# Attention scores on one core: loads issued from ScalarE's DMA queue, stores from SyncE's

## The chip, the cores and the metric

The kernel runs on one core of a Trainium2 chip. The metric is the device time of one execution in microseconds (us). The profile's span is some 2 us shorter than that time, as it leaves out what lies before the first and after the last instruction.

A profile names the engines PE (TensorE), PEld (its weight loads), DVE (VectorE), ACT (ScalarE), POOL (GpSimd) and SP (SyncE). Sixteen DMA engines move the data. "SPq" and "ACTq" are the sequencers that issue DMAs. L56 is line 56 of the kernel.

## The reference

```python
batch, heads, seq, dim = 8, 8, 512, 64          # q, k: float32
scale = 1.0 / np.sqrt(dim)
out = np.einsum('bhqd,bhkd->bhqk', q, k) * scale   # float32, (8, 8, 512, 512)
```

The inputs are 16.8 MB, the output 67.1 MB: a problem of stores.

## The kernel before

Each batch is loaded with two DMAs of 1 MB, four batches ahead. Its tiles are cast to bf16, transposed on PE, multiplied, and the scores are scaled out of PSUM, the memory that PE writes to, by ACT and DVE in turn, into output tiles of 2 MB. Six of these are in flight.

```python
raw_pool = ctx.enter_context(tc.tile_pool(name="raw", bufs=4))
out_pool = ctx.enter_context(tc.tile_pool(name="out", bufs=6))
AHEAD = 4

def load(b):
    kf = raw_pool.tile([P, 2, R * D], f32, name="kf")
    qf = raw_pool.tile([P, 2, R * D], f32, name="qf")
    nc.sync.dma_start(out=kf, in_=k_r[b])
    nc.sync.dma_start(out=qf, in_=q_r[b])
    raws[b] = (qf, kf)

load(0)
# ... identity for the transposes
for b in range(1, AHEAD):
    load(b)
# ...
for b in range(B):
    qf, kf = raws.pop(b)
    # ... casts (POOL; for b = 0 DVE and ACT), transposes, copies to kT (DVE), qT (ACT)
    for g0 in range(0, G, 2):                      # two groups a batch
        os = [out_pool.tile([P, 2 // HP, RO, S], f32, name="o") for _ in range(2)]
        # ... matmuls; evacuations alternate between ACT and DVE
        for x in range(2):
            nc.sync.dma_start(out=out_r[b, x, ...], in_=os[x]...)   # cut
        if g0 == 0 and b + AHEAD < B:
            load(b + AHEAD)
```

Of the kernel before, what the change touches and what calls it, by code (L numbers as in the profile page):

```python
# [1 line left out]

# [5 lines left out]


@with_exitstack  # L10
def kernel(
    ctx: ExitStack,
    tc: tile.TileContext,
    q: bass.AP,
    k: bass.AP,
    out: bass.AP,
):





    nc = tc.nc
    B, H, S, D = q.shape
    scale = 1.0 / (D ** 0.5)
    P = 128
    G = H // 2
    M = P // G
    R = S // M
    RO = 8  # L30
    HP = RO * P // S
    U = P // HP
    JJ = R // RO

    f32 = mybir.dt.float32
    bf16 = mybir.dt.bfloat16

    q_r = q.rearrange("b (x g) (m j) d -> b (g m) x (j d)", x=2, j=R)
    k_r = k.rearrange("b (x g) (m j) d -> b (g m) x (j d)", x=2, j=R)
    out_r = out.rearrange("b (x n h) (u i) k -> b x n (h u) i k", x=2, h=HP, i=RO)  # L40

    consts = ctx.enter_context(tc.tile_pool(name="consts", bufs=1))
    raw_pool = ctx.enter_context(tc.tile_pool(name="raw", bufs=4))
    bf_pool = ctx.enter_context(tc.tile_pool(name="bf", bufs=2))
    t_pool = ctx.enter_context(tc.tile_pool(name="t", bufs=2))
    out_pool = ctx.enter_context(tc.tile_pool(name="out", bufs=6))
    tpsum_pool = ctx.enter_context(tc.tile_pool(name="tpsum", bufs=2, space=bass.MemoryType.PSUM))
    psum_pool = ctx.enter_context(tc.tile_pool(name="psum", bufs=3, space=bass.MemoryType.PSUM))

    AHEAD = 4  # L50
    raws = {}

    def load(b):
        kf = raw_pool.tile([P, 2, R * D], f32, name="kf")
        qf = raw_pool.tile([P, 2, R * D], f32, name="qf")
        nc.sync.dma_start(out=kf, in_=k_r[b])  # L56
        nc.sync.dma_start(out=qf, in_=q_r[b])
        raws[b] = (qf, kf)

    load(0)  # L60
    identity = consts.tile([P, P], dtype=bf16)
    make_identity(nc, identity)
    for b in range(1, AHEAD):
        load(b)

    n_evac = 0

    def evacuate(dst, src):
        nonlocal n_evac
        if n_evac % 2 == 0:  # L70
            nc.scalar.mul(out=dst, in_=src, mul=scale)  # L71
        else:
            nc.vector.tensor_scalar(out=dst, in0=src, scalar1=scale, scalar2=None,  # L73
                                    op0=mybir.AluOpType.mult)
        n_evac += 1

    for b in range(B):
        qf, kf = raws.pop(b)
        kb = bf_pool.tile([P, R, 2, D], bf16, name="kb")
        qb = bf_pool.tile([P, R, 2, D], bf16, name="qb")  # L80
        for slab, dst in ((kf, kb), (qf, qb)):
            for x in range(2):
                if b > 0:
                    copy = nc.gpsimd.tensor_copy
                else:
                    copy = (nc.vector.tensor_copy, nc.scalar.copy)[x]
                copy(out=dst[:, :, x, :], in_=slab[:, x].rearrange("p (j d) -> p j d", j=R))  # L87


        kT = t_pool.tile([P, P, R], bf16, name="kT")  # L90
        qT = t_pool.tile([P, RO, P, JJ], bf16, name="qT")
        for j0 in range(0, R, 8):
            tp = tpsum_pool.tile([P, 8, P], bf16, name="tp")
            for j in range(8):
                nc.tensor.transpose(out=tp[:, j, :], identity=identity,  # L95
                                    in_=kb[:, j0 + j].rearrange("p x d -> p (x d)"))
            nc.vector.tensor_copy(out=kT[:, :, j0:j0 + 8], in_=tp.rearrange("d j p -> d p j"))  # L97
        IW = 8 // JJ
        for i0 in range(0, RO, IW):
            tp = tpsum_pool.tile([P, IW, JJ, P], bf16, name="tp")  # L100
            for i in range(IW):
                for jj in range(JJ):
                    nc.tensor.transpose(out=tp[:, i, jj, :], identity=identity,  # L103
                                        in_=qb[:, RO * jj + i0 + i].rearrange("p x d -> p (x d)"))
            nc.scalar.copy(out=qT[:, i0:i0 + IW], in_=tp.rearrange("d i jj p -> d i p jj"))  # L105

        kTh = kT.rearrange("d (g m) j -> d g (m j)", g=G)
        qTh = qT.rearrange("d i (g m) jj -> d i g (m jj)", g=G)
        for g0 in range(0, G, 2):
            os = [out_pool.tile([P, 2 // HP, RO, S], f32, name="o") for _ in range(2)]  # L110
            for n in range(2 // HP):
                for i in range(0, RO, 2):
                    pss = [psum_pool.tile([P, 2, S], f32, name="ps") for _ in range(2)]
                    for w in range(2):
                        for h in range(HP):
                            g = g0 + n * HP + h
                            for x in range(2):
                                rows = slice(x * D, (x + 1) * D)
                                nc.tensor.matmul(out=pss[x][h * U:(h + 1) * U, w, :],  # L119
                                                 lhsT=qTh[rows, i + w, g, :],  # L120
                                                 rhs=kTh[rows, g, :],
                                                 start=True, stop=True,
                                                 tile_position=(x * D, h * U))
                    for x in range(2):
                        evacuate(os[x][:, n, i:i + 2, :], pss[x])
            for x in range(2):
                n0 = g0 // HP
                nc.sync.dma_start(  # L128
                    out=out_r[b, x, n0:n0 + 2 // HP].rearrange("n p i k -> p n (i k)"),
                    in_=os[x].rearrange("p n i k -> p n (i k)"))  # L130
            if g0 == 0 and b + AHEAD < B:
                load(b + AHEAD)


# [1 line left out]
_INS = ['q', 'k']  # L136
_OUTS = [((8, 8, 512, 512), 'float32')]


# [23 lines left out]
```

## Time and profile before

| | before |
|---|---|
| time, median of 4 runs | 206.03 us |
| span of the profiled run | 204.0 us |
| PE / DVE / ACT / POOL busy | 63% / 46% / 41% / 14% |
| packets of the one data queue, share of 16 DMA engines' time | 97.6% |
| first and last of the last store's 16 completions | 198.7 and 203.2 us |

The prediction shows the lines that this rests on. The last row needs a word. A DMA is spread over the 16 DMA engines, and each reports when its part is done, so a DMA has 16 completions. The **lag** of an engine is how far its completion of the last store lies behind the first one. I sort the 16 completion times of the last store, which the trace records. They don't tell which engine is which.

### The profile page before, as it was taken

To read this page: it belongs to the slowest core of one execution; us is meant where nothing else is said; L and a number is where in the kernel's file an instruction comes from. 1 tells how busy PE (TensorE), PEld (TensorE's weight loads), DVE (VectorE), ACT (ScalarE), POOL (GpSimd) and SP (SyncE) were. 2 spreads that over 40 slices of the span, in tenths; PEclk is the share of its full clock that TensorE was granted. 3 is DMA by queue.
4 is the path that set the end of the run, shared out by engine and by line. 5 is a ranking of instruction groups with operands and counts; after the bars stand their busy time and mean duration, and the time that the engine had idled before them with its cause. 6 is when DMAs were issued, how large, how long until landed. Compare 5 with 4: busy or idle time off the path is not lost.

```text
span 204.0 us, 1911 instructions
## 1 busy us (share of the span) xinstructions
PE 128.7 (63%) x768; PEld 44.1 (22%) x768; DVE 94.4 (46%) x82; ACT 82.8 (41%) x83; POOL 29.0 (14%) x34
## 2 busy tenths in 40 slices
PE   0398877774969559696586955959787777600000
PEld 0353433260103411033110431103211111000000
DVE  0459895912639035490536705367628081800000
ACT  2477888263522625227252452527552525200000
POOL 1077530520006100070001600000000000000000
PEclk9999999666555855558555575555555555555555
DMA  5999999999999999999999999999999999999991
GB/s 204 419 409 411 439 427 404 441 434 424 437 400 432 440 421 419 434 429 427 440 407 414 438 427 437 427 421 437 424 430 437 426 434 424 430 437 427 434 408 61
DMA packets 8969, 84.01 MB, mean 412 GB/s; under 512 B 768, under 2 KB 768, under 8 KB 4864
## 3 DMA queue, kind: packets, MB, share of 16 engines
q1 hardware_dynamic: 8960, 83.89, 97.6%
q8 instruction: 6, 0.10, 0.2%
q14 instruction: 3, 0.02, 0.0%
HBM read 16.78 MB, written 67.11 MB: 411 GB/s over the span
## 4 chain that ended last, share of the span: by engine, by line
DMA 61%; DVE 14%; PE 6%; ACT 6%; issue 1%; SPq 0%; DVEq 0%
DMA out_dram<-o 57%; DVE o L73 11%; PE ps L119 4%; ACT o L71 4%; DMA qf<-in_q_dram 3%; DVE kT L97 3%; ACT qT L105 1%; PE tp L103 1%; PE tp L95 0%; DVE qb L87 0%; SPq L56 0%; SPq L128 0%; DVEq L73 0%
## 5 line engine op out<-in xcount | busy, mean ns | idle before, releaser
L119 PE MATMUL ps<-kT,qT 64*64 64x512 bf16 x512 | 103.1, 556 | 38.6 <-ACT o L71 24.9
L73 DVE TENSOR_SCALAR o<-ps 128x1024 f32<-128x1024 f32 x64 | 75.2, 1219 | 76.7 <-DMA out_dram<-o 56.8
L71 ACT ACTIVATE o<-ps 128x1024 f32<-128x1024 f32 x64 | 64.5, 1025 | 77.1 <-PE ps L119 65.7
L119 PEld LDWEIGHTS <-qT 64*64 64x64 bf16 x512 | 22.4, 124 | 111.5 <-issue 108.6
L87 POOL CAST kb<-kf 128x1024 bf16<-128x1024 f32 x14 | 14.2, 1040 | 80.9 <-DMA kf<-in_k_dram 80.3
L105 ACT COPY qT<-tp 128x1024 bf16<-128x1024 bf16 x16 | 16.1, 1015 | 12.6 <-PE tp L103 12.4
L97 DVE COPY kT<-tp 128x1024 bf16<-128x1024 bf16 x16 | 18.9, 1215 | 0.0
L95 PE MATMUL tp<-identity,kb 128*128 128x128 bf16 x128 | 12.4, 257 | 8.0 <-ACT kb L87 6.9
L103 PE MATMUL tp<-identity,qb 128*128 128x128 bf16 x128 | 14.9, 284 | 2.2 <-DVE kT L97 1.4
L87 POOL CAST qb<-qf 128x1024 bf16<-128x1024 f32 x14 | 14.2, 1040 | 6.4 <-DMA qf<-in_q_dram 6.4
L103 PEld LDWEIGHTS <-qb 128*128 128x128 bf16 x128 | 11.7, 130 | 9.6 <-issue 8.6
L95 PEld LDWEIGHTS <-kb 128*128 128x128 bf16 x128 | 10.4, 118 | 11.4 <-ACT kb L87 6.9
L87 DVE CAST kb<-kf 128x1024 bf16<-128x1024 f32 x1 | 0.7, 694 | 5.8 <-DMA kf<-in_k_dram 5.8
L87 ACT CAST kb<-kf 128x1024 bf16<-128x1024 f32 x1 | 1.0, 1044 | 3.8 <-DMA kf<-in_k_dram 3.8
L87 ACT CAST qb<-qf 128x1024 bf16<-128x1024 f32 x1 | 1.0, 1044 | 1.5 <-DMA qf<-in_q_dram 1.5
L87 ACT ACT_TABLE_LOAD x1 | 1.3, 1283 | 0.7 <-PEq L147 0.7
L87 DVE CAST qb<-qf 128x1024 bf16<-128x1024 f32 x1 | 0.7, 695 | 1.9 <-DMA qf<-in_q_dram 1.9
masks.py:199 POOL TENSOR_SCALAR_AFFINE_SELECT identity<-identity 128x128 bf16<-128x128 bf16 x1 | 0.3, 292 | 0.1
masks.py:197 POOL MEMSET identity<- 128x128 bf16 x1 | 0.2, 204 | 0.3 <-POOLq L147 0.3
L147 POOL MEMSET const-float32-0.0<- 128x1 f32 x1 | 0.1, 98 | 0.2 <-issue 0.2
L147 POOL MEMSET const-bfloat16-1.0<- 128x1 bf16 x1 | 0.1, 101 | 0.0
L147 POOL MEMSET const-uint8-127<- 128x1 uint8 x1 | 0.1, 101 | 0.0
(1 smaller groups left out, 0.1 us busy)
## 6 DMA issues: line engine op xcount, KB each, us to landing
out_dram<-o SPq DMA_DIRECT2D x32, 2048.0 KB, 24.8
kf<-in_k_dram SPq DMA_DIRECT2D x8, 1024.0 KB, 17.2
qf<-in_q_dram SPq DMA_DIRECT2D x8, 1024.0 KB, 19.6
```

What stands on the lines that cost most here:

```text
L71: nc.scalar.mul(out=dst, in_=src, mul=scale)
L73: nc.vector.tensor_scalar(out=dst, in0=src, scalar1=scale, scalar2=None, op0=mybir.AluOpType.mult)
L87: copy(out=dst[:, :, x, :], in_=slab[:, x].rearrange("p (j d) -> p j d", j=R))
L95: nc.tensor.transpose(out=tp[:, j, :], identity=identity, in_=kb[:, j0 + j].rearrange("p x d -> p (x d)"))
L97: nc.vector.tensor_copy(out=kT[:, :, j0:j0 + 8], in_=tp.rearrange("d j p -> d p j"))
L103: nc.tensor.transpose(out=tp[:, i, jj, :], identity=identity, in_=qb[:, RO * jj + i0 + i].rearrange("p x d -> p (x d)"))
L105: nc.scalar.copy(out=qT[:, i0:i0 + IW], in_=tp.rearrange("d i jj p -> d i p jj"))
L119: nc.tensor.matmul(out=pss[x][h * U:(h + 1) * U, w, :], lhsT=qTh[rows, i + w, g, :], rhs=kTh[rows, g, :], start=True, stop=True, tile_posi ...
L147: nc = _bacc.Bacc("TRN2", target_bir_lowering=False, num_devices=1)
```

## The change

Loads go to another issuer. The intent of such a change is that loads don't wait behind stores in one queue, and that SyncE has stores alone.

```diff
     def load(b):
         kf = raw_pool.tile([P, 2, R * D], f32, name="kf")
         qf = raw_pool.tile([P, 2, R * D], f32, name="qf")
-        nc.sync.dma_start(out=kf, in_=k_r[b])
-        nc.sync.dma_start(out=qf, in_=q_r[b])
+        nc.scalar.dma_start(out=kf, in_=k_r[b])
+        nc.scalar.dma_start(out=qf, in_=q_r[b])
         raws[b] = (qf, kf)
```

The compiler's scheduler then also reorders the instructions around these loads on ACT, DVE and PE.

## The prediction

> **What bounds the kernel now.** I read the page's slices first, then the DMA queues, the chain that ended last, the waits, the first 8 us of SyncE's queue, and last the packets and landings themselves.
>
> ```profile
> span 204.0 us, 1911 instructions
> ...
> PE 128.7 (63%) x768; PEld 44.1 (22%) x768; DVE 94.4 (46%) x82; ACT 82.8 (41%) x83; POOL 29.0 (14%) x34
> ...
> DMA  5999999999999999999999999999999999999991
> ...
> q1 hardware_dynamic: 8960, 83.89, 97.6%
> ...
> HBM read 16.78 MB, written 67.11 MB: 411 GB/s over the span
> ...
> DMA 61%; DVE 14%; PE 6%; ACT 6%; issue 1%; SPq 0%; DVEq 0%
> ```
>
> No compute engine is above 63%, and PE is at 63% partly because its clock is at half speed. The row of DMA is 9 from the second slice to the last but one: the 16 DMA engines never go empty in between. All loads and stores are on one queue, q1, whose packets fill 97.6% of the time of 16 engines. The chain confirms it: 61% is DMA. The rest (DVE 14%, PE and ACT 6% each) is compute that was itself let go by a store's buffer coming free, as the waits of the engines show:
>
> ```profile
> POOL kb L87 <- DMA kf<-in_k_dram: 80.3, 6, 20.0
> ...
> DVE o L73 <- DMA out_dram<-o: 56.8, 11, 8.7
> ...
> ACT o L71 <- DMA out_dram<-o: 11.1, 8, 1.7
> ```
>
> Compute waits for transfers, not transfers for compute. (POOL's 80.3 us is POOL having nothing to do; it reads far ahead of need.)
>
> How full are the DMA engines really? From the packets in the trace: 4096 load packets of 4 KB with a median of 159 ns, 4096 store packets of 16 KB with a median of 611 ns, and 768 completion packets of 9 ns. Each engine has a sixteenth: 256 x 0.159 = 40.7 us, 256 x 0.611 = 156.4 us, 48 x 0.009 = 0.4 us, in all 197.5 us. The first packet starts at 1.83 us, so an engine that never pauses ends at 199.4 us. The last store's 16 completions, one an engine, come from 198.7 to 203.2 us. So the least disturbed engine runs its packets without a gap, and the slowest is some 4.5 us behind it. The last windows (us, five engines, granted clock, DMA share, GB/s) show that tail:
>
> ```profile
> 192.00:196.00 4.00, 0.00 (x0) 0.00 (x0) 0.00 (x0) 0.00 (x0) 0.00 (x0) 0.50 0.99 426
> 196.00:200.00 4.00, 0.00 (x0) 0.00 (x0) 0.00 (x0) 0.00 (x0) 0.00 (x0) 0.50 0.76 324
> 200.00:204.00 4.00, 0.00 (x0) 0.00 (x0) 0.00 (x0) 0.00 (x0) 0.00 (x0) 0.50 0.10 41
> ```
>
> Part of that lag comes from packets that are not the kernel's data: six instruction fetches of 16 KB (queue q8) of about 1 us each, on whichever engine gets them. The floor of the kernel is thus 1.8 us of start, 197.5 us of packets, about 4 us of the slowest engine's lag, and 0.8 us after its completion: 204.
>
> **What the Trainium skill says.** "DMA: Bandwidth & Descriptors", section "Issuing engines are not separate DMA queues": DMAs from the scalar, sync or gpsimd engine run on the same 16 engines and interleave; several issuers only save the sequencer's time. The trace of before has one issuer and cannot test this, but it says that there is little issuing time to save: SyncE's queue has a median of 0.34 us for a store's issue beside 4.9 us that its 2 MB take. The same page, "Queues, rings and completion order": each engine goes round its queues packet by packet. No run here shows that yet for two data queues; it would mean that a 4 KB load packet alternates with a 16 KB store packet. "Where 436 GB/s comes from" gives a ceiling of 435 GB/s; the windows from 48 us on mostly show 418 to 442, agreeing within the way packets are counted by their start. Against these stands "Perfetto Trace Analysis", "DMA Optimizations", which says that an issuer for inputs and another for outputs may make sense, for a more dynamic spread. That pays where one waits behind the other while the DMA engines are idle, which the DMA row rules out here.
>
> **The change, part by part.**
>
> Nothing is removed: 16 loads of 1 MB and 32 stores of 2 MB, the same packets of the same sizes. The 197.5 us of packets stay.
>
> (a) The first eight loads move to ScalarE's queue. On SyncE they went like this (start, us, instruction):
>
> ```profile
> 0.74 0.43 SPq L56 DMA_DIRECT2D kf<-in_k_dram  x1
> ...
> 4.05 0.94 SPq L56 DMA_DIRECT2D kf<-in_k_dram  x1
> 5.03 2.28 SPq L57 DMA_DIRECT2D qf<-in_q_dram  x1
> ```
>
> The first begins at 0.74; ScalarE, whose first instruction (the table load) began at 0.73, can begin as early: no change of the first packet. The last one is held until 7.31, I think for room in the queue. ScalarE now does this in front of its table load (1.28 us), since the compiled order puts the eight issues first. So its first cast begins at about 7.3 + 1.3 = 8.6 us in place of 5.82: 2.8 us late. Its next load stands before the first qT copy, with a wait on POOL, at worst for the casts of batch 1 (10.96 + 2.02 = 13.0), and the one after that before the first evacuation, at worst until 13.52 + 2.02 = 15.5. The first ScalarE evacuation goes from 13.5 to about 16, and the first store from 18.9 to 21 to 22.5 us.
>
> Does the start delay the end? Only if the DMA engines run dry. The eight loads last until 8 x 2.56 + 2.8 = 23.3 us (2.56 us is the distance of two landings, 8.3 to 10.9), and the two loads issued by 16 us bring it to 28.4. That is 6 us after the first store. So 0 us.
>
> (b) The eight later loads leave SyncE's order, where each stood behind stores waiting for evacuations, and go into ScalarE's. Eight issues of about 0.4 us are 3.2 us, plus waits for buffers and for the semaphores that are shared by DMAs, on an engine that is busy 82.8 of 204 us. In the middle of the kernel ScalarE is held by full output buffers anyway. 0 us on the path.
>
> (c) Loads share the engines with stores instead of lying between them. With a 4 KB packet for each 16 KB packet, a load gets 159/(159 + 611) = 21% of the time while both wait. A batch of 2 MB then takes 5.1/0.21 = 24 us, an estimate. They are issued earlier than before, four batches ahead, so they land in time. Order changes, sums don't: 0 us.
>
> (d) The only place where the sum can move is the packet itself. The two medians give (611 - 159)/12288 = 0.0368 ns a byte and about 8 ns a packet that isn't data. If a second queue hid these 8 ns for the packets that overlap (about 128 loads and 128 stores an engine), it would save at most 2 us. If going from queue to queue costs as much, it loses 2 us. I see nothing for either sign.
>
> (e) The lag of the slowest engine depends on which engine fetches instructions when; the total stays, the spread can change by one fetch, 1 us.
>
> Sum: 0 us, give or take some 2. **206.0 us.**
>
> **The rivals.**
>
> *Loads get out of the stores' way and the kernel gains.* Before, POOL waits up to 20.0 us for a load, and ScalarE and DVE wait for stores. For it: loads are issued earlier. Against it: the DMA row has no hole to fill. Only the tail of about 4 us and the start are not full, and the change reaches neither. At best 202 to 203, still within 2%.
>
> *ScalarE becomes the bottleneck.* A load that waits in its stream holds evacuations, and a ring that is full holds them longer (the longest issue of a load was 2.28 us, of a store 4.29 us). For it: eight more such waits of 2 to 4 us are 16 to 32 us of ScalarE, in the stretch up to some 80 us. Against it: 82.8 + 32 = 115 of 204 us, and six output buffers of 2 MB are up to 29 us of stores in hand. If the stall came early, before stores pile up, the DMA engines could stop for 2 to 5 us: 208 to 211.
>
> *Mixing reads and writes packet by packet is slower.* In the mixed stretch, up to perhaps 100 us, packets of both kinds would take 3 to 5% longer, which is 3 to 5 us: 209 to 211. Before, loads and stores meet only at the borders, where the trace shows load packets of 160 to 163 ns on average in most windows, so little speaks for it.
>
> **Range and chances.** The floor holds from both sides, and the unknowns are (d), (e) and a stall at the start. Range 204.3 to 208.6. Faster by over 2% (under 201.9) would need the lag of the slowest engine gone: 0.02. Slower by over 2% (over 210.1) needs a rival at its full size: 0.05. Same: 0.93.
>
> **What the changed kernel's profile will show.** Two data queues, of 16.8 and 67.1 MB, again some 97% of 16 engines together; a DMA row of 9s; the first ScalarE cast at 8 to 9 us and the first store at 21 to 23; later loads that land before they are needed; the last store's completions spread over 3 to 5 us. A DMA row with an 8 or less between 20 and 45 us would show the early stall; a full row with a longer span and medians above 159 and 611 would show the mixing; a span shorter by more than 4 us would show that I took for a floor what is none.

## The result, and the profile after

The time is 205.25 us (205.13 to 205.38, 4 runs). The ratio to before is 0.996, with a 95% interval of 0.9942 to 0.9977. A ratio here is the mean time of one kernel's runs over that of the other's of the same rounds, so not quite the ratio of the medians quoted. The verdict is "same" at 2%, as predicted, but a gain of 0.8 us stands clear of the noise, and I had predicted none.

The page after:

```profile
span 203.2 us, 1910 instructions
...
PE 129.5 (64%) x768; PEld 46.5 (23%) x768; DVE 95.2 (47%) x82; ACT 81.9 (40%) x83; POOL 29.0 (14%) x34
...
DMA  6999999999999999999999999999999999999991
...
q1 hardware_dynamic: 4608, 67.11, 77.3%
q10 hardware_dynamic: 4352, 16.78, 20.7%
...
DMA 51%; DVE 17%; PE 14%; ACT 2%; POOL 1%; issue 1%; ACTq 1%; SPq 0%; DVEq 0%
```

The stores are alone on q1, the loads on q10, and their shares add up to 98.0%. The DMA row is as full as before. The medians of the packets are the same to the nanosecond, 159 and 611.

ACT's timeline (start, us, instruction, and what it had waited for) shows the late start that was forecast:

```profile
0.73 0.42 ACTq L56 DMA_DIRECT2D kf<-in_k_dram  x1
...
4.76 2.38 ACTq L57 DMA_DIRECT2D qf<-in_q_dram  x1
7.17 1.28 ACT L87 ACT_TABLE_LOAD   x1 [7.17 <-issue]
8.46 1.04 ACT L87 CAST kb<-kf 128x1024 bf16<-128x1024 f32 x1
...
15.80 1.94 ACT L71 ACTIVATE o<-ps 128x1024 f32<-128x1024 f32 x2 [0.66 <-PE ps L119]
```

The first cast is at 8.46 us, the first evacuation at 15.80, and the first store is issued at 23.10. None of this reaches the end of the kernel.

The end itself, in the windows of the changed kernel (us, five engines, the clock granted to TensorE as a share of full speed, DMA share, GB/s):

```profile
192.00:196.00 4.00, 0.00 (x0) 0.00 (x0) 0.00 (x0) 0.00 (x0) 0.00 (x0) 0.50 0.98 418
196.00:200.00 4.00, 0.00 (x0) 0.00 (x0) 0.00 (x0) 0.00 (x0) 0.00 (x0) 0.50 0.75 320
200.00:204.00 4.00, 0.00 (x0) 0.00 (x0) 0.00 (x0) 0.00 (x0) 0.00 (x0) 0.50 0.03 12
```

Up to 200 us these are the lines of before: 0.99, 0.76. Only the last differs, 0.03 for 0.10. The bulk of the DMA engines ends when it did; a few laggards end earlier. From the trace, the 16 lags of the last store in us:

```
before  0  .1 .2 .2 .3 .3 .4 1.0 1.0 1.5 1.5 1.6 2.5 2.9 3.6 4.5   first 198.7, sum 21.4
after   0  0  .1 .1 .1 .2 .2  .5  .8 1.4 1.5 1.5 1.5 1.6 1.7 3.7   first 198.8, sum 15.0
```

So the whole 0.8 us is the slowest DMA engine's lag, 3.7 for 4.5. The mean engine ends at 198.7 + 21.4/16 = 200.0 before and at 198.8 + 15.0/16 = 199.7 after.

Where was the mean's 0.3 us taken? Among the load packets. Leaving out the first 3 us and counting what packets of over 190 ns took beyond 159, there are 31 such packets with 6.2 us together before, and 8 with 1.3 us after. The difference of 4.9 us, over 16 engines, is 0.3 us: nearly the whole difference of the mean. The slowest engine's 0.8 us is another matter; it is traced after the experiments. Before, apart from some at 3 and 22 us, they stand at 36 to 37, 60 to 62, 86 to 87 and 107 to 113 us, where loads come after stores in the one queue.

**A surprise in the middle.** The queue of SyncE in the changed kernel (waited for: us in total, times, longest us):

```profile
SPq L128 <- ACT o L71: 109.2, 14, 12.4
SPq L128 <- DMA qf<-in_q_dram: 29.4, 3, 19.2
...
SPq L128 <- DMA kf<-in_k_dram: 18.0, 3, 10.0
```

Stores waited for loads, up to 19.2 us, although no store needs a load's data directly. The waits in the compiled program show why: each DMA uses one of eight DMA semaphores in turn, both queues share them, and a store waits until the earlier DMA of its semaphore, here a load, has landed. The windows between 56 and 72 us show what this did (engines as above):

```profile
56.00:60.00 4.00, 2.42 (x25) 0.98 (x26) 1.96 (x2) 1.62 (x2) 0.72 (x1) 0.99 0.99 409
60.00:64.00 4.00, 2.41 (x12) 0.54 (x12) 0.00 (x0) 2.37 (x3) 3.32 (x4) 0.50 1.04 429
64.00:68.00 4.00, 0.63 (x4) 0.00 (x0) 0.00 (x0) 0.00 (x0) 0.00 (x0) 0.50 1.01 429
68.00:72.00 4.00, 0.75 (x4) 0.18 (x4) 2.03 (x2) 0.00 (x0) 0.00 (x0) 0.50 1.03 437
```

From 57.5 to 62.5 us there were 498 load packets and 2 store packets: the stores were held, and the loads took the engines whole. From 64 to 72 compute almost stood still, because its output buffers came free later. The DMA share stayed at 1.0 all along, so it cost nothing.

### The profile page after: what moved, and what is told of

Same layout as the page of the kernel before. It is cut to its first block, busy times and chain, and to the rows that moved or that the text cites. A ratio compares the mean times of both kernels' runs of the same rounds, so it can differ in the third digit from the quotient of the medians.

```text
span 203.2 us, 1910 instructions
## 1 busy us (share of the span) xinstructions
PE 129.5 (64%) x768; PEld 46.5 (23%) x768; DVE 95.2 (47%) x82; ACT 81.9 (40%) x83; POOL 29.0 (14%) x34
## 4 chain that ended last, share of the span: by engine, by line
DMA 51%; DVE 17%; PE 14%; ACT 2%; POOL 1%; issue 1%; ACTq 1%; SPq 0%; DVEq 0%
DMA out_dram<-o 36%; DVE o L73 13%; DMA qf<-in_q_dram 11%; PE ps L119 10%; DVE kT L97 5%; DMA kf<-in_k_dram 4%; PE tp L95 2%; PE tp L103 2%; ACT o L71 2%; POOL kb L87 1%; ACT qT L105 1%; ACTq L56 0%; ACTq L57 0%; SPq L128 0%; DVEq L73 0%
## 5 line engine op out<-in xcount | busy, mean ns | idle before, releaser
L119 PE MATMUL ps<-kT,qT 64*64 64x512 bf16 x512 | 101.8, 584 | 35.2 <-DVE o L73 17.1
L119 PEld LDWEIGHTS <-qT 64*64 64x64 bf16 x512 | 24.0, 131 | 94.8 <-issue 91.7
L95 PE MATMUL tp<-identity,kb 128*128 128x128 bf16 x128 | 14.8, 277 | 9.6 <-ACT kb L87 9.6
L103 PE MATMUL tp<-identity,qb 128*128 128x128 bf16 x128 | 16.4, 297 | 2.5 <-DVE kT L97 1.9
L103 PEld LDWEIGHTS <-qb 128*128 128x128 bf16 x128 | 12.3, 136 | 12.5 <-issue 11.6
```

What stands on the lines that cost most here:

```text
L95: nc.tensor.transpose(out=tp[:, j, :], identity=identity, in_=kb[:, j0 + j].rearrange("p x d -> p (x d)"))
L103: nc.tensor.transpose(out=tp[:, i, jj, :], identity=identity, in_=qb[:, RO * jj + i0 + i].rearrange("p x d -> p (x d)"))
L119: nc.tensor.matmul(out=pss[x][h * U:(h + 1) * U, w, :], lhsT=qTh[rows, i + w, g, :], rhs=kTh[rows, g, :], start=True, stop=True, tile_posi ...
```

## The experiments

The theory to start with, A: the DMA engines are the bound, and only the lag of the slowest one, made by stray packets such as instruction fetches, moves the time. The rival B: two data queues as such are worth 0.4%. Twelve kernels ran, in three sets and one single; the kernels of a set ran on the same chip.

### Parts of the change, and a control

e1 swaps the issuers, e2 and e3 move only some of the loads, e4 keeps one queue but loads q ahead of k.

```diff
 # e1_swap
-                nc.sync.dma_start(     # the store
+                nc.scalar.dma_start(
 # e2_first8
-        nc.sync.dma_start(out=kf, in_=k_r[b])      # qf likewise
+        dq = nc.scalar if b < AHEAD else nc.sync
+        dq.dma_start(out=kf, in_=k_r[b])
 # e3_later8: as e2, with b >= AHEAD
 # e4_q_first
-        nc.sync.dma_start(out=kf, in_=k_r[b])
         nc.sync.dma_start(out=qf, in_=q_r[b])
+        nc.sync.dma_start(out=kf, in_=k_r[b])
```

> Loads from SyncE, stores from ScalarE: two data queues again, other issuers. Theory A (the lag of the slowest DMA engine, and it alone, sets the difference; it comes from where single extra packets such as instruction fetches fall, and any rearrangement moves it): first completion of the last store at 198.7 +- 0.3 us as in both kernels, the last one 3 to 5 us later, time 204.5 to 206.5. Rival B (two data queues as such are worth 0.4%): time 205.2, ratio 0.996, lag below 4 us like the changed kernel. Rival C (ScalarE's sequencer is hurt when it issues under full queues): over 207.

> Only the first eight loads from ScalarE: ScalarE starts late as in the changed kernel, but loads and stores never lie on two queues at the same time for long. Theory A: fast engine ends at 198.7, lag anywhere in 3 to 5 us, 204.5 to 206.5. Rival B: 206.0 (no gain, as two queues are not active together). Rival D (the late start of ScalarE costs time at the end): 207 to 209.

> Only the later eight loads from ScalarE. Rival B: 205.2, as the two queues are active together as in the changed kernel. Theory A: 204.5 to 206.5, with the first completion of the last store at 198.7 +- 0.3 and the time following the lag of the slowest engine.

> Control: one queue (SyncE) as before, but q is loaded ahead of k. No second queue, the same bytes and packets. Theory A: the time moves by up to 1 us either way although the queue is one, and the lag of the slowest engine moves with it. Rival B: 206.0 within 0.1%, ratio 1.000, lag 4.5 us.

| kernel | time, us | ratio (95%) | later loads share a queue with stores | excess of load packets over 190 ns after 30 us | first completion, slowest lag |
|---|---|---|---|---|---|
| e1_swap | 206.12 | 0.9998 (0.9977 to 1.0019) | no | 1.0 us | 202.1, 1.8 |
| e2_first8 | 205.80 | 0.9989 (0.9974 to 1.0004) | yes | 1.3 us | 199.1, 4.0 |
| e3_later8 | 205.56 | 0.9977 (0.9962 to 0.9992) | no | 0.6 us | 198.7, 3.5 |
| e4_q_first | 205.98 | 1.0001 (0.9983 to 1.0019) | yes | 5.4 us | 198.8, 4.5 |
| before | 206.05 | | yes | 4.8 us | 198.7, 4.5 |

The control e4 does not move: it has the lag of before, 4.5, and the long packets of before. That speaks against the part of A by which any rearrangement shifts the time, and for B. (The last fetch of e4 comes when that of before came, as shown below, so e4 is no test of fetches.) e3 has a gain with only the later loads moved; e2's gain is not clear of zero. In this table little excess is mostly faster and much is not, but e2 doesn't fit: it has little, and a lag of 4.0. The last part of this section says why. The count starts at 30 us; e1 has another 28 long load packets with 4.5 us at 20 to 24 us, where its stores begin beside its loads. And e1 has two queues as well and gains nothing. Its profiled run is the slowest of its six (206.67 us). The page and two windows show another loss:

```profile
DMA  5999999999999999999989999999999999999994
...
96.00:100.00 4.00, 1.85 (x12) 0.53 (x12) 0.76 (x1) 2.93 (x4) 0.00 (x0) 0.50 0.92 389
100.00:104.00 4.00, 3.60 (x29) 1.70 (x25) 1.80 (x3) 2.67 (x3) 0.00 (x0) 0.50 0.66 281
```

Here the DMA engines ran dry, with a share of 0.66 from 100 to 104 us. What ACT waited for (us in total, times, longest) tells why it was late with its work:

```profile
ACT o L71 <- DMA out_dram<-o: 17.5, 1, 17.5
ACT qT L105 <- DMA kf<-in_k_dram: 14.3, 1, 14.3
```

ACT, which had to evacuate, stood behind its own store issues, one of which waited for a load's semaphore. This is the rival "ScalarE becomes the bottleneck" of the prediction, and with stores on ACT it is real. Yet it cost little. The first completion comes 3.4 us later than before (202.1), but the lag is 1.8 in place of 4.5: while the fast engines had nothing, the slow ones caught up. The largest lag of a store was 2.0 us at 97 us, and 0.2 at 109. A pause in the middle is paid for with lag, up to the lag that would have been there.

### Transfers alone

e5 and e6 keep the loads and stores and drop everything else; the stores read one cleared tile. Their outputs are wrong, which doesn't matter for the times. e7 is the real kernel with 128 tiny memsets a batch on POOL, which was meant to add instruction fetches.

```diff
 # e5_dma_one; e6_dma_two: the same with nc.scalar in load()
+    src = consts.tile([P, 2 // HP, RO, S], f32)
+    nc.vector.memset(src, 0.0)
-            # casts, transposes, matmuls, evacuations
-                    in_=os[x].rearrange(...))
+                    in_=src.rearrange(...))
 # e7_pool
+        for _ in range(128):
+            nc.gpsimd.memset(scratch, 0.0)
         kT = t_pool.tile([P, P, R], bf16, name="kT")
```

> Wrong results on purpose: the same 16 loads and 32 stores on SyncE's queue, stores from one cleared tile, no other work. Theory A: no instruction fetches of the compute engines, so all 16 DMA engines keep step: the last store's completions within 0.6 us, first at 198.7 +- 0.5, span 199.5 to 200.5, time about 202. Rival E (some DMA engines are slower by nature): the lag of 4 to 5 us stays, span 203 to 204.

> The same with the loads on ScalarE's queue. Theory A: equal to the one-queue version within 0.2 us, so a second data queue neither hides nor costs packet time: about 202, lag below 0.6 us. Rival B: 0.8 us faster than the one-queue version. Rival F (mixing packet by packet is slower): 2 us or more slower.

> The kernel before plus 1024 tiny POOL memsets on an idle engine, some 100 us of POOL work beside 29. Results stay right. Theory A: 1024 more instructions are some four more fetches of 16 KB (six before), each about 1 us on one DMA engine: the first completion of the last store stays at 198.7 to 199.0, the sum of the 16 engines' lags rises from 21 us by 3 to 8, and the slowest engine's lag goes from 4.5 to 4.5 to 6.5: time 206.0 to 208. Rival E: no change, 206.0.

**e5:** 203.04 us, ratio 0.9859 (0.9844 to 0.9874); first completion 199.0, slowest lag 1.5, sum 10.8. Neither of the two expectations was met. Without compute 3 of the 4.5 us of lag are gone, so the engines are not slow by nature. But 1.5 us are left with no instruction fetch in the run. The load packets over 190 ns show where they come from: 43 of them, 11.8 us together, in clusters at 22, 36, 61, 86 and 110 us, just where loads follow stores. From this I formed **theory G**: in one queue, the border from stores to loads stretches packets.

**e6:** 203.69 us, ratio 0.9879 (0.9857 to 0.9902), with runs from 202.94 to 205.34. The profiled run is the one of 205.34. There the slowest lag was 0.2, but the first completion came at 202.5, as the engines ran dry at 112 to 114 us:

```profile
DMA  5999999999999999999999799999999999999997
...
SPq L84 <- DMA kf<-in_k_dram: 76.1, 7, 17.6
```

The 7 in the DMA row is the pause, and the wait below is the shared semaphores again: the stores of this kernel depend on nothing but them and one early memset, and still waited 76.1 us for kf loads. So two queues are no gain of themselves; they can lose by this coupling what they gain. Nor do they keep load packets short: after 3 us, e6 has 82 long ones with 17.6 us, more than e5, and 58 of them lie at 6 to 10 us, where its stores begin. Theory G, which speaks of one queue, has no answer to that.

**e7** failed as a test. It took 258.7 us, ratio 1.2562 (1.2544 to 1.2581), because the memsets delayed the casts on POOL, which became the chain:

```profile
POOL 48%; issue 18%; PE 11%; DVE 7%; ACT 4%; DMA 3%; POOLq 1%; DVEq 0%; SPq 0%
```

It says nothing of what fetches do to the lag, as the engines paused often in it, and again ended with little lag, 1.8. It does show fetches: the forecast four more of 16 KB did not come, but its page has 11 of 8 KB on another queue, q14, where before has 3.

### Borders and fetches

e8 puts all loads ahead of all stores, one border in the harmless direction. e9 puts a load of 0.5 MB after each store. e10 is the real kernel with one queue and twice as many borders. e11 is the changed kernel again.

```diff
 # e8_loads_first (from e5)
-    for b in range(1, AHEAD):
+    for b in range(1, B):
         load(b)
-            if g0 == 0 and b + AHEAD < B:
-                load(b + AHEAD)
 # e9_alternate (from e5): no load() calls, and after each store
+                nc.sync.dma_start(out=half[:, x], in_=in_r[b][:, x])
 # e10_split_one (from before); load() is cut into load_k() and load_q()
             if g0 == 0 and b + AHEAD < B:
-                load(b + AHEAD)
+                load_k(b + AHEAD)
+            if g0 == 2 and b + AHEAD < B:
+                load_q(b + AHEAD)
```

> Wrong results on purpose: transfers only, one queue, all 16 loads ahead of all 32 stores, so the queue goes from loads to stores once and never back. Theory G (in one queue, a load that follows a store has stretched packets, up to 0.8 us; the one-queue transfers-only kernel had 11.8 us of this over 16 engines in loads longer than 190 ns at its four or five borders): almost no load packets over 190 ns after the start, sum of lags below 4 us, span 200 to 200.6, time 201.9 to 202.4. If the borders are innocent: as the other one-queue version, 203.0, sum of lags about 11 us.

> Wrong results on purpose: transfers only, one queue, after each 2 MB store a load of 0.5 MB, some 28 borders where there were five. Theory G, at the 2.4 us a border of the other version: about 65 us of stretched packets over 16 engines, 4 us each: span 203.5 to 206, time 205 to 208. If the borders are innocent: 203 (at most 0.3 us for 16 more completions).

> The real kernel, one queue, results right; of the later batches, k is loaded after the first group and q after the second, so each later batch makes two borders in place of one. Theory G: long load packets (over 190 ns) rise from 6 us to 8 to 14 us in sum, mean lag by 0.2 to 0.5 us, time 206.0 to 206.8, at any rate not faster. Borders innocent: 206.0 with the same 6 us.

> The changed kernel again, on this chip beside the others: ratio 0.996 +- 0.002 if its 0.8 us is the kernel's own; 1.000 if it was chance or one chip's. Theory G: load packets over 190 ns sum below 2.5 us (before: 6.2).

**e8:** 202.09 us, ratio 0.9808 (0.9796 to 0.9821). One load packet over 190 ns, all 16 completions within 0.2 us. Against e5, which moves the same bytes on the same queue in another order, the borders cost about 1 us (203.04 less 202.09, from two sets). This is what theory G forecast.

**e9:** 207.94 us, ratio 1.0094 (1.0081 to 1.0107). The time is at the upper edge of what G expected, but not in the way expected. The long load packets sum to 11.6 us, no more than in e5, while 111 store packets over 640 ns take 32.8 us too long, many of them by exactly 597 ns. And the cost is not spread: eleven engines lag 0.5 us at most, five lag 5.5 to 5.7, a value that they reach between 50 and 110 us and keep.

**e10:** 208.31 us, ratio 1.0125 (1.0104 to 1.0145), correct results, and beyond the 206.0 to 206.8 expected. The long load packets sum to 12.6 us, as expected, but again on few engines: the lags end with 3.0, 5.2, 6.1 and 8.0. (The profiled run is the slowest of six, 209.49 us.) The tail of its profile has 0.21 where the changed kernel has 0.03:

```profile
196.00:200.00 4.00, 0.00 (x0) 0.00 (x0) 0.00 (x0) 0.00 (x0) 0.00 (x0) 0.50 0.75 320
200.00:204.00 4.00, 0.00 (x0) 0.00 (x0) 0.00 (x0) 0.00 (x0) 0.00 (x0) 0.50 0.21 90
```

The fastest engine ended as ever (first completion 198.7). The slowest alone made the kernel longer, by 2.2 us in the median. The lags of 6.1 and 8.0 were reached by 121 us, among the last loads, and stayed.

**e11:** 205.25 us, ratio 0.9961 (0.9948 to 0.9974), slowest lag 3.7, long load packets 1.3 us. The gain of the change repeats.

What was left of theory A, the instruction fetches, was tried with a clean kernel: e8 plus as many TensorE instructions as the real kernel has, for which nobody waits.

```diff
 # e12_pe_fetch (from e8)
+    for _ in range(192):
+        tp = tpsum_pool.tile([P, 8, P], bf16, name="tp")
+        for j in range(4):
+            nc.tensor.transpose(out=tp[:, j, :], identity=identity, in_=identity)
```

> Wrong results on purpose: the loads-first transfers-only kernel (202.1 us, all 16 DMA engines within 0.2 us at the end) plus 768 transposes of the identity that nobody reads: TensorE gets as many instructions as in the real kernel, and no other engine waits for them. Theory A (instruction fetches make the lag): six fetches of 16 KB on q8 come back, about 6 us in sum and some 3 us of stretched stores beside them; sum of lags from 1.7 to 8 to 12 us, slowest engine 1.3 to 3 us behind, time 203.2 to 205. If the lag comes from the compute engines' use of SBUF instead: 202.1, lag 0.2, as these transposes read one small tile.

**e12:** 203.42 us, ratio 0.9874 (0.9857 to 0.989), so 1.3 us over e8. The page has the fetches back:

```profile
q8 instruction: 6, 0.10, 0.2%
```

The lags are 0.4 us or less for ten engines, and 1.5, 1.6, 1.6, 1.6, 1.7 and 1.7 for six. Six fetches, six engines: each fetch of 16 KB puts one engine back by about 1.6 us, more than the fetch packet's own 1.03 to 1.09 us. Here no engine got two.

### The slowest engine, followed back

Besides the six fetches of 16 KB on q8, which the prediction counted, the real kernels fetch 8 KB at a time on q14. The pages before and after:

```profile
q14 instruction: 3, 0.02, 0.0%
...
q14 instruction: 2, 0.02, 0.0%
```

In the changed kernel the third one comes after the end. The next table follows the largest lag through the kernel, by the store whose first completion came at about the time in the head (us):

| kernel | 155 | 165 | 175 | last store | third fetch on q14 at |
|---|---|---|---|---|---|
| before | 3.59 | 4.30 | 4.48 | 4.49 | 162.3 |
| e4_q_first | 3.54 | 4.29 | 4.48 | 4.50 | 162.4 |
| e2_first8 | 2.98 | 3.19 | 3.93 | 3.95 | 173.4 |
| after | 3.25 | 3.47 | 3.65 | 3.65 | 205.2 |
| e11_after_again | 3.36 | 3.56 | 3.74 | 3.75 | 205.2 |
| e3_later8 | 3.14 | 3.35 | 3.52 | 3.52 | 203.3 |

In each of them one engine falls back a little with nearly every store until compute ends at about 180 us; in e5 and e8, without compute, and e12, with TensorE's alone, none does. (In before, the 3.59 is another engine's; the one that falls back stood at 3.53.) Where the third fetch comes before the last store, the largest lag jumps by some 0.6 us at that moment; where it comes after, there is no jump. This explains e2. In before the fetch took 309 ns, and the store packet that starts as it ends 880 ns, which is 269 over the median. So of the 0.84 us of lag between before and after, about 0.6 is one fetch of 8 KB that no longer comes in time to matter. The other 0.2 to 0.3 stays open.

The borders held back other engines, on top of the 1.5 us or so of a 16 KB fetch: before, three of these stand at about 2.5, 2.9 and 3.6 from 116 us to the end; after, none is over 1.7.

Why does the fetch come later? It comes when SyncE has started 79 to 83 of the instructions that the trace records for it in before, e2, e3, e4 and e10, and in the changed kernel SyncE has 76 in all. So it looks like a piece of SyncE's own program, which the loads have made shorter by leaving it. No run tests this.

No version beat the changed kernel. Loads-first, which is best for the transfers, would have to hold all eight batches before the first store; in this kernel it was not built.

## Why the prediction was right, and what it missed

**The bound** was named rightly. The medians of the packets did not change, the first completion moved by 0.1 us, and the DMA row stayed full. Take all compute away (e8) and 202.1 us are left of 206.

**(a) The late start.** First cast at 8.46 us (8.6 forecast), first ScalarE evacuation at 15.80 ("about 16"), first store at 23.10, a little after the 21 to 22.5 given. No cost at the end, as said. e2, which has this late start alone, is not slower than before (205.80).

**(b) Loads in ScalarE's stream.** No cost, and its busy time is 81.9 us for 82.8. The rival behind it does show in e1, where ScalarE issues the stores. What the step missed: it foresaw waits for shared semaphores in ScalarE's stream, but not for the stores in SyncE's.

**(c) Sharing.** From 35 to 55 us there were 438 load packets to 413 store packets, and the loads had 22% of the engines' time, for the 21% estimated: packet for packet. This agrees with what the Trainium skill says in "DMA: Bandwidth & Descriptors", section "Queues, rings and completion order". But "order changes, sums don't: 0 us" was wrong by 0.3 us on the mean engine. Order does change the sum: there are 4.9 us of stretched load packets less over 16 engines. I had looked at these packets, saw means of 160 to 163 ns in most windows, and took that for nothing. A mean hides it, since the excess sits in 21 packets after 30 us and on few engines.

**(d) The fixed 8 ns of a packet** were neither hidden nor doubled: medians of 159 and 611 in both kernels. The rival that mixing reads and writes is slower packet by packet is refuted by the same numbers.

**(e) The lag of the slowest engine** was allowed 1 us, by where a fetch falls, with no sign given, and the 0.8 us came there. In the main this is what happened: about 0.6 us is one fetch that no longer comes before the last store. The prediction knew only the six fetches on q8, which are six in both kernels, and not the three on q14. And "the total stays" was wrong: the sum of the 16 lags fell from 21.4 to 15.0 us, most of it by border packets on engines that did not end last. The sign of the change was not foreseen.

The part that the borders play in the time is clear where they are doubled (e10, a lag of 8.0), and not in the change itself: there they explain the mean's 0.3 us, and at most the 0.2 to 0.3 us of the slowest engine that the fetch leaves over. Without compute, e5 against e8, they cost about 1 us.

Several things stay open. Packets are not labelled by engine, so what each engine lost is read from the sorted lags. No run moves the fetch alone. Why one engine falls back while compute works, why a border stretches packets, or why in e9 just five engines suffered and stopped at 5.7 us, no run tells.

## What to carry to other kernels

Where the DMA row has no hole, moving transfers to another issuer can hardly be worth more than the lag of the slowest DMA engine (an inference from these runs), so read that lag from the last transfer's completions before hoping for gains. In one queue, keep loads and stores in long runs, as returns from stores to loads can cost, and on few engines: doubling them cost 2.2 us of 206. Before a small gain is credited to the idea of a change, look where the instruction fetches fall: parting the queues won 0.8 us, and about 0.6 of it is one fetch that came later. Put the loads, not the stores, on an engine that also computes, and check in the compiled waits which transfers share semaphores, since with two queues a store can end up waiting for a load it has nothing to do with.

## What the Trainium skill lacked or had wrong

- "DMA: Bandwidth & Descriptors", section "Issuing engines are not separate DMA queues": it says that several issuers only save the sequencer's issue time. Parting loads from stores gave 0.996 twice. This is no clear counter-example, as about 0.6 of the 0.8 us go with one instruction fetch. The page has nothing on load packets that are stretched where loads follow stores in one ring (6.2 us in sum before, 1.3 after); with more such borders, e9 lost 5.9 us (against e8) and e10 2.2 us (against before).
- The same page, section "Queues, rings and completion order": packet for packet agrees (438 to 413), but the page does not spell out that this leaves 4 KB loads only 22% of the time beside 16 KB stores.
- "Runtime: NRT & Kernel Launch", section "Instruction fetch mechanics", has the fetches of 16 KB on a DMA queue, but not what they cost the transfers beside them: in e12 six of them for 768 matmuls and their weight loads each put one DMA engine back by 1.5 to 1.7 us, 1.3 us on the time. Nor does it have the fetches of 8 KB seen here, one of which put an engine back by about 0.6 us.
- "DMA: Bandwidth & Descriptors", section "Latency and other measured facts", has a row on two DMA engines that are usually slower. It lacks that one engine falls back while compute works (by 3.5 us or more at the end in the real kernels that never pause, where all 16 end within 0.2 us in e8), and that a pause lets the engines close up: from 2.0 to 0.2 us in e1.
- "Perfetto Trace Analysis", section "DMA Optimizations": separate issuers for inputs and outputs, especially with loops or control flow, "to allow more dynamic spread". The spread was bound by the shared semaphores: stores waited for loads up to 19.2 us in the changed kernel, and transfers alone were not faster with two issuers than with one (203.69 and 203.04 us).
